# Token order and weight-slot columns in an RWKV-7 / short-convolution layer: every moving slice starts on a multiple of 512 bytes

## The chip, the cores and the metric

The kernel runs on one core of a Trainium2 chip. Five engines work side by side: PE (TensorE, with a second row "PEld" for its weight loads), DVE (VectorE), ACT (ScalarE), POOL (GpSimd) and SP (SyncE, which issues most DMAs). The metric is the device time of one execution in microseconds; the figure of a kernel is the median of its runs.

## The reference, cut to what matters

512 real tokens of width 2048 follow 16 learned meta tokens, so that the layer sees 528. They are normalised and multiplied by one wide matrix `w_in` (2048 x 8320); its columns feed two branches.

```python
h_res = jnp.concatenate([meta, x], axis=1)            # 16 + 512 tokens
hn = _rmsnorm(h_res, norm_in_g[l])
P = hn @ w_in[l]
Pr, Pc = P[..., :RW_COLS], P[..., RW_COLS:]
prev = jnp.pad(Pr[:, :-1], ((0, 0), (1, 0), (0, 0)))
Pr = Pr + (prev - Pr) * mu_shift[l]                   # r, k, v, g, low-rank parts
...
y = _rwkv7_recurrence(rh, decay, kh, vh, kk, kk * ah) # 16 meta frames, then chunks of 64
...
y_b = Bg * _causal_depthwise_conv(Cg * hc, conv_w[l]) * jax.nn.silu(g_c)
mix = jnp.concatenate([y_a, y_b], axis=-1)
h_res = h_res + mix @ w_out[l]
out = _rmsnorm(h_res, norm_f_g)
return out[:, N_META:]
```

Two things of it decide which tokens a column group needs. k, v and the low-rank input ("lora") feed the state from the first meta token on, so they need all 528. r and g need the 512 real tokens and one before them for the shift; C and h need the real tokens and two before them for the convolution of width 3; B and the gate gc need the real tokens alone.

## The kernel before

**The projection.** The 8320 columns of `w_in` are 65 tiles of 128. One tile's product is called a piece: lora, and k, r, v, g, B, C, h, gc with index 0 to 7. `plan` (lines 102 to 107) is their order. The moving operand is the normalised-gain input, split into a high part `xh` and a low part `xl` of 16 rows (one for each 128 input features) of `XROW` = 640 floats, 2560 bytes, of which 528 are tokens. The stationary operand is a 128x128 block of the weights, likewise split into `hi` and `lo`. A block's product is three matmuls, (hi, xh), (hi, xl), (lo, xh), each with a weight load of its own. `steps` (line 320) issues them: for each quarter of a piece (4 of the 16 input rows), for each token range, for each row, the three matmuls.

**Token ranges.** A range is a slice of the moving row and has its own PSUM bank. Tokens lie in time order, meta tokens first. Lines 315 to 318 hold them: `FULL` for k, v and lora, `TAIL` for r and g, `WIDE` for C and h, `REAL` for B and gc. A piece of two ranges has 96 matmuls of 256 to 272 columns, one of `REAL` 48 of 512.

**Weight slots.** Each quarter's weights stand in one of six buffers of `SLOT` = 1152 floats, 4608 bytes (`slot`, line 124): 512 floats of hi and then 512 of lo, shifted inside the slot by `column(j)` floats, which depends on the piece (lines 115 to 119). Rows of 2560 bytes, slots of 4608 and blocks of 512 are all multiples of 512 bytes, so within a piece the distance between where a moving slice begins and where its weights begin is the same modulo 512 bytes for every matmul of a range. In this text **the distance** of a range is (start of the slice - column) x 4 bytes, modulo 512, with the bases of the two pools taken as a multiple of 512 bytes apart.

**Weights on the way.** SP loads half a piece (512 KB) at a time into one of three raw buffers; `split_w` (line 134) casts a quarter to hi on ACT (line 136) and subtracts on DVE or POOL (line 137).

**Out of PSUM.** `scaled` (line 346) multiplies a range by the tokens' norm factors `rs` on DVE, one instruction a range (line 348), and writes a row in time order. `shift_full` and `shift_real` then mix each token with the one before it (ACT and DVE); `use` sends C and h through a product on POOL and the convolution.

**Order.** PE runs in the order in which the program is written; the other engines' order is made by a planner when the kernel is built. The generator `mains` yields one projection matmul at a time, and `fill(ns)` takes projection matmuls until their estimated time (0.43 ns a column) is used up, between the small matmuls of the RWKV branch (lines 563 to 1003). So the projection is what PE does while the branch's chain of DVE, ACT, POOL and DMA steps runs. After the last piece, gc7, a second phase multiplies the mixed branches by `w_out` (line 1234).

**Head.** The first four pieces, lora, k0, r0 and B0, run interleaved while the input arrives. `token_scale_sums` and `token_scale` make `rs`.

Of the kernel before, what the change touches and what calls it, by code (L numbers as in the profile page):

```python
# [13 lines left out]
ALU = mybir.AluOpType  # L14
# [7 lines left out]
SEQ = 512  # L22
META = 16
L = SEQ + META
# [53 lines left out]
def hymba_kernel(ctx: ExitStack, tc: tile.TileContext, xt, xtok, front, w_in, w_out, pv, lup, cst, msk, gf, out):  # L78
    nc = tc.nc
# [35 lines left out]
    def column(j):  # L115
        what, i = plan[j]
        return {
            "k": 8 * i, "v": 8 * i + 56, "r": 8 * i, "g": 8 * i + 56, "C": 8 * i, "h": 8 * i + 56, "B": 8 * i, "gc": 8 * i + 56, "lora": 0,
        }[what]
    stream += [w_out[0, g] for g in range(3)]  # L120
    quarters, chain, low = {}, {}, {}
# [35 lines left out]
    rs = xp.tile([P, L], F32, name="rs")  # L157
# [79 lines left out]
    o = 0  # L237
# [61 lines left out]
    with tc.issue_after(head):  # L299
        nc.vector.tensor_scalar(  # L300
            out=omm, in0=pvt[:, V_MU : V_MU + 33], scalar1=-1.0, scalar2=1.0, op0=ALU.mult, op1=ALU.add
# [10 lines left out]
        )  # L312

    nc.scalar.copy(ones, cs[:, C_BM : C_BM + P + 2])
    FULL = ((0, 256), (256, L))
    TAIL = ((14, 270), (270, L))
    WIDE = ((14, 272), (272, L))
    REAL = ((META, L),)

    def steps(ps, ranges, k4, q, ks=range(4), rs_=range(2)):  # L320
        hi, lo = quarters[q]
# [23 lines left out]

    def scaled(ranges, ps, dst, base):
        for (a, b), p in zip(ranges, ps):
            nc.vector.tensor_tensor(out=dst[:, a - base : b - base], in0=p, in1=rs[:, a:b], op=ALU.mult)

    def shift_full(ps, m, name, dst):  # L350
        pr = cq.tile([P, L + 1], F32, tag="pr", name=f"pr_{name}", bufs=2)
# [42 lines left out]
    def use(what, i, ps):  # L394
        if what == "lora":
            use_lora(ps)
        elif what in ("k", "v"):
            t = cq.tile([P, LP], F32, tag=what, name=f"{what}{i}")
            nc.gpsimd.memset(t[:, META:CH], 0.0)
            shift_full(ps, tile_of[what] + i, f"{what}{i}", padded(t))  # L400
            got[what, i] = t
        elif what in ("r", "g"):
            t = cq.tile([P, SEQ], F32, tag=f"r{i % 2}" if what == "r" else "g", name=f"{what}{i}")
            shift_real(ps, tile_of[what] + i, f"{what}{i}", t)
            if what == "g":
                gate(t, f"r{i}")
                later(14000, lambda: nc.sync.dma_start(gated[i], t))
            got[what, i] = t
        elif what == "C":
            u = tm(f"u{i}")  # L410
            scaled(WIDE, ps, u, 14)
            got[what, i] = u
        elif what == "h":
            u = got["C", i]
            hh = tm(f"hh{i}")
            with behind_of("turned"):
                scaled(WIDE, ps, hh, 14)
            n = SEQ + 2
            nc.gpsimd.tensor_tensor(out=u[:, 0:n], in0=u[:, 0:n], in1=hh[:, 0:n], op=ALU.mult)
            cv = tp.tile([P, SEQ], F32, tag="cw", name=f"cv{i}")  # L420
            nc.scalar.activation(cv, u[:, 0:SEQ], AF.Copy, scale=col(V_CW, i))
            for j in (1, 2):
                nc.vector.scalar_tensor_tensor(
                    out=cv, in0=u[:, j : j + SEQ], scalar=col(V_CW, 8 * j + i), in1=cv, op0=ALU.mult, op1=ALU.add
                )
            got[what, i] = cv
            if i == 0:
                nc.gpsimd.tensor_tensor(out=cv, in0=cv, in1=got["B", 0], op=ALU.mult)
        elif what == "B":
            b = tm(f"b{i}")[:, 0:SEQ] if i else cq.tile([P, SEQ], F32, name="b0")  # L430
            with behind_of("split"):
                scaled(REAL, ps, b, META)
            got[what, i] = b
            if i:
                nc.gpsimd.tensor_tensor(out=got["h", i], in0=got["h", i], in1=b, op=ALU.mult)
        else:
            cv = got["h", i]
            g = tm(f"gc{i}")[:, 0:SEQ]
            scaled(REAL, ps, g, META)
            gate(g, f"c{i}")  # L440
            o = direct.get(8 + i, cv)
            nc.vector.scalar_tensor_tensor(out=o, in0=cv, scalar=0.5, in1=g, op0=ALU.mult, op1=ALU.mult)
            if o is cv:
                later(9000, lambda: nc.sync.dma_start(mixd[8 + i], cv))
        ready.add((what, i))
# [29 lines left out]
    def mains():  # L475
        pa = banks(FULL, "lora", pm, "main")
        pb = banks(FULL, "k0", pz, "tz")
        pc = banks(TAIL, "r0", pm, "main")
        pd = [pi.tile([P, SEQ], F32, tag="ser", name="ps_B0")]
        four = ((pa, FULL), (pb, FULL), (pc, TAIL), (pd, REAL))  # L480
        for k in range(4):
            for n, (ps, rg) in enumerate(four):
                if k == n == 0:
                    hi, lo = quarters[0]
                    for ww, xx, first in ((hi, xh, True), (lo, xh, False), (hi, xl, False)):
                        for p, (a, b) in zip(ps, rg):
                            nc.tensor.matmul(p, ww[:, 0:P], xx[:, 0, a:b], start=first, stop=False)
                            yield (b - a) * 0.43
                    continue
                yield from steps(ps, rg, 0, 2 * n, (k,))  # L490
        for k4 in range(1, 4):
            for n, (ps, rg) in enumerate(four):
                h = 4 * (k4 // 2) + n
                if k4 == 2:
                    prefetch(h + 3)
                if (k4, n) == (3, 2):
                    yb = token_scale_sums()
                if (k4, n) == (3, 3):
                    yield from steps(ps, rg, k4, 2 * h + k4 % 2, range(2))
                    token_scale(yb, 4)  # L500
                    use("lora", 0, pa)
                    use("k", 0, pb)
                    yield from steps(ps, rg, k4, 2 * h + k4 % 2, range(2, 4))
                    continue
                for r in range(2 if n < 3 else 1):
                    if (k4, n, r) == (3, 2, 1):
                        token_scale(yb, 0)
                    yield from steps(ps, rg, k4, 2 * h + k4 % 2, range(4), (r,))
        use("r", 0, pc)
        use("B", 0, pd)  # L510
        for j in range(4, len(plan)):
            what, i = plan[j]
            rg = FULL if what in ("k", "v") else REAL if what in ("B", "gc") else WIDE if what in ("C", "h") else TAIL
            ps = yield from main(j, rg, f"{what}{i}")
            if what == "B" and i < 4:
                state["split"] = low[4 * j + 4]
            use(what, i, ps)
# [794 lines left out]
    for half in range(2):  # L1312
        o = 28 * half
        for g in range(4):
            b = o + 4 + 4 * g
# [134 lines left out]
def _layout(i):  # L1450
    f = np.float32
    x = np.asarray(i["x"])[0]
    hres = np.concatenate([np.asarray(i["meta_tokens"]), x], 0)
    xt = hres.reshape(L, KT, P).transpose(2, 1, 0)
    w = np.asarray(i["w_in"])[0].reshape(KT, P, 65, P).transpose(2, 1, 0, 3).reshape(65, P, DM)

    w, xv, xo = np.array(w), slice(16, 32), slice(0, NPAIR)
    w[xv] = w[xv].reshape(16, P, KT, 2, CH)[:, :, :, ::-1].reshape(16, P, DM)
    wo = np.array(np.asarray(i["w_out"])[0].reshape(KT, 2, CH, 4, 512))
    wo[xo] = wo[xo][:, ::-1]  # L1460
    wo = wo.reshape(8, 2, P, 4, 512).transpose(3, 0, 2, 1, 4).reshape(4, 8, P, 1024)

    def cols(a):
        return np.asarray(a).reshape(-1, P).T

    def swapped(a, first, last):
        a = np.array(cols(a))
        a[:, first:last] = np.roll(a[:, first:last], CH, 0)
        return a

    cw = np.asarray(i["conv_w"])[0]
    pv = np.concatenate(
        [cols(i["norm_in_g"]), swapped(i["mu_shift"], 16, 32)]
        + [cols(i[n]) for n in ("w0", "a0", "k_k", "k_a")]
        + [swapped(i[n], 0, NPAIR) for n in ("lnx_g", "lnx_b")]
        + [cols(i["r_k"])]
        + [cols(cw[j]) for j in range(3)],
        1,
    )
    lup = np.stack([np.asarray(i[n])[0].reshape(64, 8, P) for n in ("w_lora_up", "a_lora_up")], 2)  # L1480
    lup = np.concatenate([lup, lup], 0).transpose(1, 0, 2, 3)

    first = [w[m, :, 0:512].reshape(P, 4, P) for m in (32, 8, 0, 33)]
    front = [pv[:, V_NG : V_NG + KT], first[0][:, 0], xt[:, 0]] + [t[:, 0] for t in first[1:]]
    front += [t[:, 1] for t in first] + [xt[:, 1]] + [t[:, 2:4].reshape(P, 256) for t in first] + [xt[:, 2], xt[:, 3]]
    front = np.concatenate(front, 1)
    cst, msk = _constants()
    return dict(
        xt=xt, xtok=x, front=front, w_in=w, w_out=wo, pv=pv, lup=lup, cst=cst, msk=msk, gf=np.asarray(i["norm_f_g"])
    )  # L1490
# [19 lines left out]
```

## Time and profile before

| | us |
|---|---|
| runs of the kernel | 1026.65, 1027.34, 1027.67 |
| their median | 1027.34 |
| the profiled execution | 1025.72 |
| its span, first to last instruction | 1024.0 |

The mean granted TensorE clock of the profiled execution is 0.998. A row of a group of instructions reads: line, engine, operation, out<-in by the program's names, shapes, count, then busy microseconds and mean nanoseconds of one, then the engine's idle time just before them with what ended it. Matmul durations are modelled and overlap, so a matmul's real price is read from start to start, here called its **pitch**. In the chain of waits a row is start, length and work, and consecutive matmuls of one tile stand as one row with their count; length over count is the pitch. In the timeline a row is start, length, engine, line, operation, tiles, shape and count.

### The profile page before, as it was taken

How to read it: one execution, taken by the hardware profiler on the slowest of the kernel's cores; microseconds unless marked ns; L12 is line 12 of the kernel's file. 1: busy time of each engine (PE TensorE's matmuls, PEld its weight loads, DVE VectorE, ACT ScalarE, POOL GpSimd, SP SyncE). 2: the span in 40 equal slices, each digit the busy share in tenths (PEclk: the TensorE clock that was granted, in tenths of full speed). 3: DMA queues.
4: the chain of work that ended last, by engine and by line, in shares of the span. 5: the costliest groups of instructions: out<-in, count | busy, mean ns of one | idle time of the engine just before them, and what ended most of it. 6: DMA issues, size and time to landing. Idle time of an engine off the chain costs nothing.

```text
span 1024.0 us, 23688 instructions
## 1 busy us (share of the span) xinstructions
PE 1005.1 (98%) x9723; PEld 920.1 (90%) x9723; DVE 685.2 (67%) x1239; ACT 393.4 (38%) x729; POOL 281.2 (27%) x292
## 2 busy tenths in 40 slices
PE   9999999999999999999999999999999999999996
PEld 8899998999988999998999998989889897787875
DVE  7677965587765569555569554244555696998787
ACT  7553423344323434322434322222222335545453
POOL 0122323233232323322423222123332332005001
PEclk9999999999999999999999999999999999999999
DMA  9525576446574363864264855977673697695754
GB/s 324 155 69 145 124 191 173 116 118 150 134 188 130 103 172 88 215 167 117 83 163 100 219 140 166 347 238 232 202 223 95 180 274 180 179 319 139 177 126 165
DMA packets 185036, 174.82 MB, mean 171 GB/s; under 512 B 121568, under 2 KB 142816, under 8 KB 184416
## 3 DMA queue, kind: packets, MB, share of 16 engines
q1 hardware_dynamic: 182336, 164.40, 55.6%
q0 software_dynamic: 2304, 8.39, 4.9%
q8 instruction: 76, 1.25, 0.5%
q10 hardware_dynamic: 288, 0.52, 0.1%
q14 instruction: 32, 0.26, 0.1%
HBM read 136.92 MB, written 36.35 MB: 169 GB/s over the span
## 4 chain that ended last, share of the span: by engine, by line
PE 56%; DVE 8%; DMA 3%; issue 2%; ACT 0%; POOL 0%; DVEq 0%; ACTq 0%; SPq 0%; POOLq 0%
PE ps_gc L329 8%; PE ps_B L329 7%; PE ps_h L329 7%; PE ps_C L329 7%; PE ps_v L329 5%; PE ps_k L329 5%; PE ps_g L329 5%; PE ps_r L329 4%; DVE o L1207 3%; DMA wo<-in_w_out_dram 2%; PE M L1234 2%; PE zs L999 1%; PE zy L1003 1%; PE g L674 1%; DVE xb L1215 1%
## 5 line engine op out<-in xcount | busy, mean ns | idle before, releaser
L137 POOL TENSOR_TENSOR w<-wr,w 128x512 fp32r<-128x512 f32 x119 | 172.2, 1448 | 367.6 <-ACT w L136 307.5
L136 ACT CAST w<-wr 128x512 fp32r<-128x512 f32 x252 | 153.1, 618 | 302.9 <-PE ps_k L329 47.7
L137 DVE TENSOR_TENSOR w<-wr,w 128x512 fp32r<-128x512 f32 x133 | 98.3, 745 | 109.4 <-ACT w L136 98.2
L329 PE MATMUL ps_k<-xh,w 128*128 128x256 f32 (+1 forms) x512 | 96.8, 285 | 1.1 <-DVE w L137 1.1
L329 PE MATMUL ps_v<-xh,w 128*128 128x272 f32 (+1 forms) x512 | 96.5, 285 | 0.0
L329 PE MATMUL ps_r<-xh,w 128*128 128x256 f32 (+1 forms) x512 | 96.4, 283 | 0.0
L329 PE MATMUL ps_h<-xh,w 128*128 128x256 f32 (+1 forms) x512 | 95.2, 284 | 0.0
L329 PE MATMUL ps_C<-xh,w 128*128 128x256 f32 (+1 forms) x512 | 94.1, 282 | 0.0
L329 PE MATMUL ps_g<-xh,w 128*128 128x258 f32 (+1 forms) x512 | 93.4, 282 | 0.0
L329 PE MATMUL ps_B<-xh,w 128*128 128x512 f32 x256 | 84.5, 399 | 0.0
L329 PE MATMUL ps_gc<-xh,w 128*128 128x512 f32 x256 | 82.6, 397 | 0.0
L329 PEld LDWEIGHTS ps_k<-xh,w 128*128 128x128 f32 x512 | 80.4, 188 | 1.8 <-DVE w L137 1.4
L329 PEld LDWEIGHTS ps_r<-xh,w 128*128 128x128 f32 x512 | 80.4, 189 | 0.3
L329 PEld LDWEIGHTS ps_v<-xh,w 128*128 128x128 f32 x512 | 80.4, 188 | 0.3
L329 PEld LDWEIGHTS ps_h<-xh,w 128*128 128x128 f32 x512 | 79.6, 188 | 1.1 <-issue 0.3
L329 PEld LDWEIGHTS ps_C<-xh,w 128*128 128x128 f32 x512 | 79.5, 188 | 0.6
L329 PEld LDWEIGHTS ps_g<-xh,w 128*128 128x128 f32 x512 | 79.4, 189 | 0.3
L329 PE MATMUL ps_v<-xl,w 128*128 128x256 f32 (+1 forms) x256 | 72.8, 284 | 0.0
L329 PE MATMUL ps_k<-xl,w 128*128 128x256 f32 (+1 forms) x256 | 72.8, 284 | 0.0
L329 PE MATMUL ps_g<-xl,w 128*128 128x256 f32 (+1 forms) x256 | 72.6, 284 | 0.0
L329 PE MATMUL ps_r<-xl,w 128*128 128x256 f32 (+1 forms) x256 | 72.4, 283 | 0.0
L329 PE MATMUL ps_h<-xl,w 128*128 128x258 f32 (+1 forms) x256 | 71.9, 281 | 0.2 <-issue 0.2
(321 smaller groups left out, 2272.6 us busy)
## 6 DMA issues: line engine op xcount, KB each, us to landing
wr<-in_w_in_dram SPq DMA_DIRECT2D x126, 512.0 KB
ct<-opd SPq DMA_DIRECT2D x64, 288.0 KB
wo<-in_w_out_dram SPq DMA_DIRECT2D x24, 512.0 KB
x<-in_w_out_dram POOLq DMA_DIRECT2D x16, 512.0 KB, 5.8
opd<-ar SPq DMA_DIRECT2D x8, 576.0 KB
opd<-gt SPq DMA_DIRECT2D x16, 288.0 KB
opd<-bt SPq DMA_DIRECT2D x64, 64.0 KB
x<-in_w_out_dram SPq DMA_DIRECT2D x8, 512.0 KB
```

Source lines behind the costliest of these rows:

```text
L136: nc.scalar.copy(hi, rq)
L137: low[q] = eng.tensor_tensor(out=lo, in0=rq, in1=hi.bitcast(F32), op=ALU.subtract).ins
L329: nc.tensor.matmul(ps[r], ww[:, w], xx[:, kt, a:b], start=(kt == 0 and n == 0), stop=(kt == KT - 1 and n == 2))
L674: nc.tensor.matmul(z[h][:, c - c0], bk[hs, c, h : h + 2, :].rearrange("p a s -> p (a s)"), ar[hs, c].rearrange("p a s -> p (a s)"), start= ...
L999: nc.tensor.matmul(d[hs, j], w, x[hs], start=(a == 0), stop=(a == b - 1))
L1003: nc.tensor.matmul(d[ho, j], t[hs, o : o + CH], x[hs], start=(a == 0), stop=(a == b - 1))
L1207: nc.vector.tensor_tensor(out=lo, in0=rq, in1=hi.bitcast(F32), op=ALU.subtract)
L1215: nc.vector.tensor_tensor(out=h, in0=h, in1=ps, op=op)
L1234: nc.tensor.matmul(bank[s], left(prod, jj, m, s), w, start=(jj == 0 and n == 0), stop=(jj == 7 and n == 2))
```

## The change

The tokens are laid out with the 512 real ones first, then the last two meta tokens, then the first fourteen. Every range now begins at 0 or at 256 floats, a multiple of 512 bytes. The ranges keep 256 + 272 columns for k, v and lora, 256 + 258 for r and g, and 512 for B and gc; C and h, which had 258 + 256, take `TAIL` too and have 256 + 258. `scaled` cuts each range where the token order jumps, so that rows behind it are in time order as before: two ranges of `FULL` take four instructions in place of two, `TAIL` three in place of two, `REAL` one as before. Weight slots are shifted by 16 floats for k, v and lora, by 0 for B and gc, by 8 i for r and C and by 8 i + 64 for g and h.

```diff
@@ column(j)
-            "k": 8 * i, "v": 8 * i + 56, "r": 8 * i, "g": 8 * i + 56, "C": 8 * i, "h": 8 * i + 56, "B": 8 * i, "gc": 8 * i + 56, "lora": 0,
+            "k": 16, "v": 16, "lora": 16, "B": 0, "gc": 0,
+            "r": 8 * i, "g": 8 * i + 64, "C": 8 * i, "h": 8 * i + 64,
@@ ranges
-    FULL = ((0, 256), (256, L))
-    TAIL = ((14, 270), (270, L))
-    WIDE = ((14, 272), (272, L))
-    REAL = ((META, L),)
+    HALF = SEQ // 2
+    FULL = ((0, HALF), (HALF, L))
+    TAIL = ((0, HALF), (HALF, SEQ + 2))
+    REAL = ((0, SEQ),)
+    PLACED = ((0, SEQ, META), (SEQ, SEQ + 2, META - 2), (SEQ + 2, L, 0))
@@ def scaled(ranges, ps, dst, base)
         for (a, b), p in zip(ranges, ps):
-            nc.vector.tensor_tensor(out=dst[:, a - base : b - base], in0=p, in1=rs[:, a:b], op=ALU.mult)
+            for c, d, t in PLACED:
+                c0, d0 = max(a, c), min(b, d)
+                if c0 < d0:
+                    o = t + c0 - c - base
+                    nc.vector.tensor_tensor(
+                        out=dst[:, o : o + d0 - c0], in0=p[:, c0 - a : d0 - a], in1=rs[:, c0:d0], op=ALU.mult
+                    )
@@ use, mains: C and h
-            scaled(WIDE, ps, u, 14)
+            scaled(TAIL, ps, u, 14)
...
-            rg = FULL if what in ("k", "v") else REAL if what in ("B", "gc") else WIDE if what in ("C", "h") else TAIL
+            rg = FULL if what in ("k", "v") else REAL if what in ("B", "gc") else TAIL
@@ def _layout(i)
-    hres = np.concatenate([np.asarray(i["meta_tokens"]), x], 0)
+    meta = np.asarray(i["meta_tokens"])
+    hres = np.concatenate([x, meta[META - 2 :], meta[: META - 2]], 0)
```

The distances that follow, in bytes, by the definition above (i is the piece's index):

| pieces | before, the two ranges | after, both ranges |
|---|---|---|
| lora, k | 512 - 32 i | 448 |
| v | 288 - 32 i | 448 |
| r | 56 - 32 i | 512 - 32 i |
| g | 344 - 32 i | 256 - 32 i |
| C | 56 - 32 i, 64 - 32 i | 512 - 32 i |
| h | 344 - 32 i, 352 - 32 i | 256 - 32 i |
| B | 64 - 32 i | 0 |
| gc | 352 - 32 i | 0 |

(each modulo 512). The moving slices of r, g and the first of C and h began at 56 or 1080 bytes, those of B and gc at 64.

More of the change, by code (lines that the diff above doesn't have):

```diff
@@ L416, in use @@
             with behind_of("turned"):
-                scaled(WIDE, ps, hh, 14)
+                scaled(TAIL, ps, hh, 14)
             n = SEQ + 2
```

## The prediction

> **What bounds the kernel now.** I read the page, then the busy time by stage, then PE's waits.
>
> ```profile
> span 1024.0 us, 23688 instructions
> ...
> PE 1005.1 (98%) x9723; PEld 920.1 (90%) x9723; DVE 685.2 (67%) x1239; ACT 393.4 (38%) x729; POOL 281.2 (27%) x292
> ```
> ```profile
> 56.00:170.00 114.00, 113.50 (x919) 109.37 (x917) 80.61 (x166) 42.60 (x80) 33.19 (x39) 1.00 0.56 140
> 170.00:330.00 160.00, 157.31 (x1682) 149.40 (x1683) 110.70 (x216) 58.38 (x109) 51.55 (x55) 1.00 0.54 144
> 330.00:630.00 300.00, 300.00 (x2804) 286.68 (x2804) 188.82 (x382) 105.74 (x193) 91.52 (x92) 1.00 0.54 141
> 630.00:811.00 181.00, 180.76 (x2988) 160.22 (x2986) 83.61 (x139) 49.76 (x94) 54.50 (x46) 1.00 0.71 221
> 811.00:857.00 46.00, 46.00 (x292) 41.52 (x291) 39.68 (x55) 16.23 (x31) 16.76 (x10) 1.00 0.86 232
> ```
> ```profile
> PE t L846 <- DVE xn L837: 2.0, 1, 2.0
> ...
> PE ps_k L329 <- DVE w L137: 1.1, 1, 1.1
> ```
>
> The columns of the second view are stretch, length, PE, PEld, DVE, ACT and POOL busy (with counts), granted clock, DMA share, GB/s. From 56 to 857 us PE is busy in 797.6 of 801 us at a granted clock of 1.00, and its two longest waits are 2.0 and 1.1 us. No other engine comes near. The matmuls' pitch sets this stretch, so a nanosecond on a projection matmul goes to the end. What follows hangs on the last piece:
>
> ```profile
> 844.90 11.17 PE ps_gc L329 x48
> ...
> 856.09 0.69 DVE gc L348
> ...
> 859.04 5.49 DMA x<-in_w_out_dram
> ```
>
> In the chain of waits gc7 frees DVE at 856.09, and after the gate a DMA is issued at 859.04 for which the second phase waits. An earlier gc7 moves all of this earlier.
>
> **The pitch, and what the distance does to it.** These are rows of the chain; length over count is the pitch.
>
> ```profile
> 328.31 11.79 PE ps_k L329 x96
> ...
> 341.67 2.40 PE ps_r L329 x20
> ...
> 352.61 8.70 PE ps_v L329 x72
> ...
> 392.16 11.78 PE ps_v L329 x96
> ...
> 458.24 8.16 PE ps_B L329 x35
> ...
> 471.25 8.83 PE ps_gc L329 x37
> 480.08 11.73 PE ps_k L329 x96
> ...
> 543.83 11.73 PE ps_v L329 x96
> ...
> 609.87 8.36 PE ps_B L329 x35
> ...
> 622.98 8.62 PE ps_gc L329 x37
> 631.60 11.41 PE ps_C L329 x96
> ...
> 799.56 11.24 PE ps_gc L329 x48
> 810.80 11.44 PE ps_C L329 x96
> 822.25 11.44 PE ps_h L329 x96
> 833.69 11.21 PE ps_B L329 x48
> ```
>
> B2 (458.24) and B3 (609.87) are cut at the same points by the same small matmuls; only the distance differs, 0 against 480 bytes. The pitch is 233.1 against 238.9 ns. gc3 (622.98, distance 256) against gc2 (471.25, 288) gives 233.0 against 238.6. So the pitch does depend on the distance, by 5.7 ns in 235. The Trainium skill, "SBUF — State Buffer", section "Who interferes with whom", gives PE two independent read ports, one for the moving operand and one for weight loads, and says that PE never waits on anyone; by it the distance would do nothing. The two pairs disagree, and the measurement decides.
>
> With 256 columns the pitch has several stable values:
>
> ```profile
> 145.22 0.28 PE L329 MATMUL ps_C<-xl,w 128*128 128x256 f32 x1
> ...
> 146.24 0.28 PE L329 MATMUL ps_C<-xl,w 128*128 128x256 f32 x1
> ```
> ```profile
> 172.05 0.29 PE L329 MATMUL ps_k<-xl,w 128*128 128x272 f32 x1
> ...
> 173.17 0.29 PE L329 MATMUL ps_k<-xl,w 128*128 128x272 f32 x1
> ...
> 173.88 0.28 PE L329 MATMUL ps_k<-xl,w 128*128 128x256 f32 x1
> ...
> 174.59 0.28 PE L329 MATMUL ps_k<-xl,w 128*128 128x256 f32 x1
> ...
> 178.05 0.28 PE L329 MATMUL ps_k<-xl,w 128*128 128x256 f32 x1
> ...
> 178.73 0.28 PE L329 MATMUL ps_k<-xl,w 128*128 128x256 f32 x1
> ```
>
> Every third matmul reads xl, so between two such rows lie 9, 9, 6 and 6 matmuls. C0 (distance 64) runs at 1.02/9 = 113 ns. k2 already stands where the change puts all of k and v, at 448 bytes with column 16 and ranges from 0 and 256: its 272 columns take 1.12/9 = 124 ns, its 256 columns 0.71/6 = 118 ns in one group and 0.68/6 = 113 ns in another, the latter just after small matmuls had broken in. One distance thus holds two rhythms, and which one holds depends on what ran before.
>
> **The sum, part by part.**
>
> B and gc go to distance 0. B2 and gc3 have that pitch already; 13 pieces gain 5.7 ns x 48 = 0.27 us each: **3.5 us**. The least I take is 2.5 (some of the 13 are near it already), the most 4.0.
>
> k and v: k4, k6, v5 and v7 take 11.79, 11.73, 11.78 and 11.73, mean 11.76 us. At k2's values a piece is 48 x (118 + 124) = 11.62 us in the slower rhythm and 48 x (113 + 124) = 11.38 in the faster; halfway, 11.50, gains 0.26. v4 (352.61) has 120.8 ns, 11.60 a piece, and is no worse than the middle; with k2, k3 and v3, which stand at or within one step of 448 or of v4's 160, I count it as nothing. 11 pieces x 0.26 = **2.8 us**; ends 1.5 and 4.2.
>
> r and g begin at 56 bytes now and have 120 ns whatever the width (341.67: 2.40/20). C and h have one such range and one of 256 columns on a multiple of 64 bytes, and 11.41 and 11.44 us a piece, a pair of 238.3 ns, so the aligned range has about 118.3. After the change r and g are built like that. 15 pieces (r0 is in the head) x 48 x 1.7 ns = **1.2 us**. For 258 columns from 256 no row exists; the nearest are k's 272 columns (124 ns, which at equal excess is 118) and the unaligned 120. I take 120, since their mean over distances is nearer it. Ends: 31 pieces x 48 x 2 ns, 3.0 us either way. C0 loses its 113: 48 x 5 ns = **-0.25 us**.
>
> The head: lora, k0 and B0 are of the same kind, 2 x 0.26 + 0.27 = 0.8 us, of which I count half, **0.4**, as the wait for `rs` stands behind them.
>
> DVE gets 2 more instructions for each of 17 pieces and 1 more for each of 32: 66. The nearest row is a copy of 16 columns out of PSUM:
>
> ```profile
> L473 DVE COPY rs<-prs 128x16 f32<-128x16 f32 x1 | 0.2, 174 | 0.2 <-PE prs L472 0.2
> ```
>
> At 0.174 us that is 11.5 us of DVE time at most, against 1024.0 - 685.2 = 338.8 idle. It lies beside PE's next piece (11 us); a PSUM bank is written again two pieces later. If that cover were gone, all 11.5 us would show. No DMA and no wait of SP's or POOL's queue is moved.
>
> Not all of PE's gain survives, since other engines' steps do not shrink:
>
> ```profile
> 61.54 0.70 DVE L387 TENSOR_TENSOR la<-lora_th,la 64x528 fp32r<-64x528 f32 x1
> ```
> ```profile
> 62.30 0.39 PE L564 MATMUL tz<-la,luh 128*128 128x272 f32 x1
> ```
>
> DVE ends `la` at 62.24 and PE takes it at 62.30: v0's share before it, 52 matmuls x 2.6 ns, becomes a wait of 0.15 us, and lora's and k0's four small pieces may add 0.4. Before the 2.0 us wait for xn nothing on PE since the last gram matmuls (37 us before) helps: 0.9% of 37, 0.3 us. Together **-0.8 us**, ends 0 and 3.
>
> Sum: 3.5 + 2.8 + 1.2 - 0.25 + 0.4 - 0.8 = 6.85 us, 0.7%. The profiled span goes from 1024.0 to 1017.2; its execution has 1.7 us around it, 1018.9; the median of the runs lies 1.6 above that execution: **1020.5 us**.
>
> **The rivals.**
>
> *The distance is worth less than the pairs say.* The pairs were measured with slices that began at 64 bytes and columns that were not 0; if only B and gc answer, and k and v stay in the slower rhythm, 3.5 us remain less 0.5 of waits: **1024.3**. For it: k2's first groups at 118 ns. Against it: v4's 120.8.
>
> *The distance does nothing for the end.* PE saves, and waits for DVE steps that have not moved: **1027.3**. For it: the matmul at 62.30 comes at once behind `la`. Against it: the 300 us from 330 to 630 without any idle time. The port rule quoted above would end here too; the pairs speak against it.
>
> *Every rhythm is the fast one.* With 256 columns at 113 ns throughout (C0, k2), k and v gain 4.2, and r, g, C and h 46 x 48 x 5 = 11 us: with half of the latter, 3.5 + 4.2 + 5.5 - 1, **1015**. The Trainium skill, "TensorE: Matmul & The Clock Gate", section "Back-to-back issue gap", has N/2.4 + 2.5 ns, 109 ns for 256 columns; no row here gets below 113.
>
> *Slower: weights come late.* The planner puts the added DVE pieces ahead of weight splits on DVE; PE then starves as k2 did at 1.1 us (line 137, in the waits above). Each such stall costs 1.1 us, so from seven on the gain is gone; at ten the time is 1020.5 + 11, **1031.5**. Against it: PE leaves a quarter every 2.9 us (11.7/4) and six buffers stand between, so a split of 0.7 us must be some 10 us late.
>
> **How the numbers follow.** The forecast (gain 4 to 10 us) has 0.60, the weak gain 0.14, nothing 0.09, every rhythm fast 0.08, slower 0.09. What a measurement of this kernel can tell from no change is about 0.2%, 2 us. Faster is 0.60 + 0.14 + 0.08 = 0.82, same 0.09, slower 0.09. The parts' ends, 2.5 + 1.5 - 1.8 and 4.0 + 4.2 + 4.2 before waits, and the neighbours put the range at **1015.5 to 1026**; beyond it lie the slower case and parts of two others.
>
> **What would show it.** B's and gc's pitch in stretches without breaks is near 233 or less in every piece; whole k and v pieces take 11.4 to 11.6 us; r and g come to 11.4; PE still shows no wait over 2 us before 857. It is wrong if B's pitch stays at 234 or more, if 258 columns exceed 121 ns, or if PE waits for line 137 or 348 appear by the dozen.

## The result, and the profile after

| | median, us | runs | ratio to before, with its 95% interval |
|---|---|---|---|
| before | 1027.51 | 1026.65 to 1028.28 (4) | |
| after | 1022.37 | 1021.18 to 1022.86 (4) | 0.9948 [0.9931, 0.9966] |

The change saves 5.1 us, half a per cent. The profiled execution of after took 1022.35 us; against the profiled execution of before, 1025.72, that is only 3.4 us. The two differ in the granted clock as well, 0.995 against 0.998, and this will matter below.

First the head of the page of after and its busy time by stage (stretch, length, then busy PE, PEld, DVE, ACT and POOL, granted clock, DMA share, GB/s).

```profile
span 1020.6 us, 23761 instructions
...
PE 1001.5 (98%) x9723; PEld 919.9 (90%) x9723; DVE 688.1 (67%) x1305; ACT 393.9 (39%) x729; POOL 274.8 (27%) x292
```
```profile
170.00:330.00 160.00, 157.56 (x1678) 149.63 (x1679) 110.83 (x228) 57.70 (x109) 46.28 (x55) 0.99 0.54 144
330.00:630.00 300.00, 300.00 (x2822) 286.93 (x2821) 191.43 (x411) 107.00 (x196) 91.20 (x92) 1.00 0.54 143
```

PE still sets the time. It has as many matmuls as before, is still busy in all 300 us from 330 to 630, and does 2822 of its records there in place of 2804: the same work at a shorter pitch. DVE has the 66 added instructions and only 2.9 us more busy time than before. In the stage before, the clock is 0.99 and no longer 1.00.

Then the rows of the chain of waits (start, length, work) that answer to those of before.

```profile
328.76 11.58 PE ps_k L331 x96
...
341.92 2.39 PE ps_r L331 x20
...
352.87 8.65 PE ps_v L331 x72
...
392.06 11.54 PE ps_v L331 x96
...
457.53 8.16 PE ps_B L331 x35
...
470.48 8.62 PE ps_gc L331 x37
479.10 11.59 PE ps_k L331 x96
...
542.04 11.53 PE ps_v L331 x96
...
607.68 8.16 PE ps_B L331 x35
...
620.61 8.62 PE ps_gc L331 x37
629.23 11.55 PE ps_C L331 x96
...
797.47 10.89 PE ps_gc L331 x48
808.35 11.36 PE ps_C L331 x96
819.72 11.36 PE ps_h L331 x96
831.08 10.90 PE ps_B L331 x48
841.98 10.89 PE ps_gc L331 x48
```

B2 and B3 both take 8.16 us now, gc2 and gc3 both 8.62; before, one of each pair was slower. Whole B and gc pieces take 10.89 or 10.90 where they took 11.17 to 11.24: 226.9 ns a matmul against 233 to 234. k and v come from 11.73 to 11.79 down to 11.53 to 11.59. C and h are no better as a group: C4 (629.23) went up from 11.41 to 11.55, C7 and h7 down from 11.44 to 11.36. gc7 ends at 852.87, 3.2 us earlier than the 856.07 of before.

PE's waits (engine, what waits, for whom; us in all, times, longest):

```profile
PE t L854 <- DVE xn L845: 2.2, 1, 2.2
...
PE ps_k L331 <- DVE w L138: 1.1, 1, 1.1
PE ps_h L331 <- issue: 0.8, 1, 0.8
...
PE ps_gc L331 <- DVE w L138: 0.2, 1, 0.2
```

No wait for weights by the dozen has appeared. The wait for `xn` went from 2.0 to 2.2 us; h6's 0.8 and gc's 0.2 are small. What the waits do not show stands behind the first of them, in PE's timeline (start, length, work; in brackets the wait):

```profile
306.81 1.12 PE L854 MATMUL t<-xn,gt 64*64 64x64 f32 x32 [2.17 <-DVE xn L845]
...
307.86 0.79 PE L331 MATMUL ps_B<-xh,w 128*128 128x512 f32 x1
...
308.45 0.63 PE L331 MATMUL ps_B<-xl,w 128*128 128x512 f32 x1
308.88 1.05 PE L331 MATMUL ps_B<-xh,w 128*128 128x512 f32 x2
309.73 0.63 PE L331 MATMUL ps_B<-xl,w 128*128 128x512 f32 x1
```

From 308.45 to 309.73 lie three matmuls: 427 ns each instead of 228. The granted clock is halved for 3.4 us from 306.9, and once more for 3.4 us from 863.3, behind a wait of 1.7 us for ACT, which had itself waited for a DMA. The profile of before has neither, although its wait for `xn` was nearly as long (2.01 us).

### The profile page after: what moved, and what is told of

It is laid out like the page before. It is cut to its first block, busy times and chain, and to the rows that moved or that the text cites. A ratio compares the mean times of both kernels' runs of the same rounds, so it can differ in the third digit from the quotient of the medians.

```text
span 1020.6 us, 23761 instructions
## 1 busy us (share of the span) xinstructions
PE 1001.5 (98%) x9723; PEld 919.9 (90%) x9723; DVE 688.1 (67%) x1305; ACT 393.9 (39%) x729; POOL 274.8 (27%) x292
## 4 chain that ended last, share of the span: by engine, by line
PE 56%; DVE 8%; DMA 3%; issue 3%; ACT 1%; POOL 0%; DVEq 0%; ACTq 0%; SPq 0%; POOLq 0%
PE ps_gc L331 8%; PE ps_B L331 7%; PE ps_h L331 7%; PE ps_C L331 7%; PE ps_v L331 5%; PE ps_g L331 5%; PE ps_k L331 5%; PE ps_r L331 4%; DVE o L1215 3%; DMA wo<-in_w_out_dram 2%; PE M L1242 2%; PE zs L1007 1%; PE zy L1011 1%; PE rz L955 1%; PE g L682 1%
## 5 line engine op out<-in xcount | busy, mean ns | idle before, releaser
L138 POOL TENSOR_TENSOR w<-wr,w 128x512 fp32r<-128x512 f32 x119 | 165.4, 1390 | 368.7 <-ACT w L137 317.1
L331 PE MATMUL ps_h<-xh,w 128*128 128x258 f32 (+1 forms) x512 | 95.3, 284 | 0.0
L331 PE MATMUL ps_C<-xh,w 128*128 128x258 f32 (+1 forms) x512 | 94.4, 283 | 0.0
L331 PE MATMUL ps_h<-xl,w 128*128 128x256 f32 (+1 forms) x256 | 72.2, 282 | 0.8 <-issue 0.8
```

What stands on the lines that cost most here:

```text
L138: low[q] = eng.tensor_tensor(out=lo, in0=rq, in1=hi.bitcast(F32), op=ALU.subtract).ins
L331: nc.tensor.matmul(ps[r], ww[:, w], xx[:, kt, a:b], start=(kt == 0 and n == 0), stop=(kt == KT - 1 and n == 2))
```

## The experiments

"Steady pitch" is my own evaluation of the traces: the mean of start to start of consecutive projection matmuls in stretches without breaks, by piece and width. The "excess" of a kernel is the sum over all these pairs of (pitch - columns/2.4), in us; it is what the pitch costs beyond streaming. Before has 64.86 us of it, after 58.97.

**Before once more, unchanged.** How much of a profile's difference is chance?

> The kernel before, unchanged, for a second profile. If its first profiled execution (1025.72 us, clock 1.00 throughout) was a lucky one, this one is near 1027.5 us and shows one or two stretches of some 3.4 us at half clock behind PE's waits near 305 and 865 us, some 1.3 us each, as the changed kernel's profile does. If the clock is not what separates them, it shows no such stretch and the same projection pitches, and the 1.8 us lie elsewhere.

One run: 1025.16 us, span 1023.4, clock 0.997. The excess is 64.85 us against 64.86 in the first profile of before, and there is no stretch at half clock. Before's summed pitch thus repeats to 0.01 us, and that of after, which was profiled twice as well (58.97 and 59.22), to 0.25. The time of a run does not repeat as well: 15 runs of before taken beside this one go from 1026.12 to 1028.30. A second measure that repeats is the time from v0's first matmul to gc7's last, here called the **main stretch**: 799.62 and 799.63 us in the two profiles of before. v0's first matmul itself starts at 56.04 and 55.73, so the head moves by 0.3 us by chance.

**The distance alone, without the new order.** The tokens stay in time order, ranges begin where they did, `scaled` is the old one; only the columns change, so that k, v and lora stand at 448 bytes, B and gc at 0, r and g at 448, C and h at 440 (258 columns) and 448 (256).

```diff
@@ against before
-            "k": 8 * i, "v": 8 * i + 56, "r": 8 * i, "g": 8 * i + 56, "C": 8 * i, "h": 8 * i + 56, "B": 8 * i, "gc": 8 * i + 56, "lora": 0,
+            "k": 16, "v": 16, "lora": 16, "B": 16, "gc": 16,
+            "r": 30, "g": 30, "C": 32, "h": 32,
```

> The old token order and ranges, only the columns changed: k, v, lora, B and gc to 16, so that k and v keep distance 448 and B and gc distance 0 with slices that begin at 64 bytes; r and g to 30 (distance 448 from starts at 56 bytes), C and h to 32 (440 and 448). Distance theory: B and gc at 227 to 229 ns, k and v at 113 to 118 and 123.5 ns, the gain of the change is here too, about 5.5 us, 1022 us; C's and h's aligned range gains 1 to 3 ns more (up to 2 us); r and g stay at 120 ns or fall to 116 if an even start does not matter. Rival, that slices must begin on multiples of 512 bytes: B and gc stay near 233 ns and the time near 1027.

1021.14 us (1019.78 to 1022.94, 5 runs), 0.9937 [0.9924, 0.9951]. The excess is 58.97, the same as after's. The main stretch takes 796.07 us, in the profile of after above 796.56. This profile too has the two stretches at half clock, from 306.6 and 863.0, so the new order is not needed for them. From its chain of waits:

```profile
328.34 11.58 PE ps_k L330 x96
...
391.60 11.53 PE ps_v L330 x96
...
796.36 10.88 PE ps_gc L330 x48
807.24 11.40 PE ps_C L330 x96
...
830.05 10.91 PE ps_B L330 x48
840.95 10.90 PE ps_gc L330 x48
```

k, v, B and gc are as fast as in after, with B's slices at 64 bytes and k's row order untouched. So the columns give as much as the whole change, without the new token order and the 66 DVE instructions. One thing the distance does not do here: r and g, whose slices begin at 56 and 1080 bytes, stay at 120 ns at distance 448, where C's and h's 256 columns, which begin at 1088 bytes, have 116.5 and 116.7.

**The order alone.** After, with the columns of before.

```diff
@@ against after
-            "k": 16, "v": 16, "lora": 16, "B": 0, "gc": 0,
-            "r": 8 * i, "g": 8 * i + 64, "C": 8 * i, "h": 8 * i + 64,
+            "k": 8 * i, "v": 8 * i + 56, "r": 8 * i, "g": 8 * i + 56, "C": 8 * i, "h": 8 * i + 56, "B": 8 * i, "gc": 8 * i + 56, "lora": 0,
```

> The new token order and ranges with the old columns. Distance theory: B and gc keep a mean of 232 ns, k and v of 118 and 125.4; r and g fall from 120 to 118 ns in their 256 columns (-1 us) and the 258 columns rise by 1 ns (+1.3 us): no change, 1027 to 1028 us. Rival, that starts on 512 bytes bring the gain: 1022.4 us.

1026.19 us (1024.46 to 1028.63, 11 runs), 0.9993 [0.9984, 1.0002]: no difference that can be told. The excess is 64.02, 0.8 below before; the main stretch takes 799.30 us, 0.3 below before. Its chain:

```profile
327.77 11.80 PE ps_k L330 x96
...
391.67 11.78 PE ps_v L330 x96
...
799.02 11.19 PE ps_gc L330 x48
...
833.14 11.19 PE ps_B L330 x48
```

The k, v, B and gc pieces have the lengths of before. The order does bring r's and g's 256 columns from 120.1 to 117.9 and 117.5 ns, but their 258 columns, now from float 256, go from 119.5 to 120.1. It also carries the 66 added DVE instructions of after, and shows that they cost nothing that can be told.

**All of r, g, C and h at 448.** After, with one column for them.

```diff
@@ against after
-            "r": 8 * i, "g": 8 * i + 64, "C": 8 * i, "h": 8 * i + 64,
+            "r": 16, "g": 16, "C": 16, "h": 16,
```

> The changed kernel with r, g, C and h at column 16 too, distance 448 in all pieces of two ranges. Distance theory: their 256 columns fall from a mean of 118 ns to the 114 to 116 that C2, h2 and r2 show at 448 and 192, 31 pieces x 48 x 3 ns = 4 us, so 1018 us. Rival, that C2 and r2 are good by what runs before them and not by distance: 1022.4 us.

1018.22 us (1017.24 to 1018.89, 4 runs), 0.9913 [0.9899, 0.9926]; excess 54.56. That is 4.4 us of pitch below after. C's, g's and h's 256 columns run at 114.5 to 114.9 ns, r's at 116.1; the 258 columns stay at 120.3. Over the sixteen distances of the change the mean is 117.7 to 118.3, so they cost against one good one. Beside the columns-only kernel it shows what moving the starts off 56 and 1080 bytes does at the same distance of 448: r's and g's 256 columns go from 120.2 and 120.1 ns to 116.1 and 114.9.

**A sweep of distances.** Each piece a column of its own; B and gc cover 15 distances of 512 columns, r, g, C and h others of 256.

```diff
@@ against after
-            "k": 16, "v": 16, "lora": 16, "B": 0, "gc": 0,
-            "r": 8 * i, "g": 8 * i + 64, "C": 8 * i, "h": 8 * i + 64,
+            "k": 16, "v": 16, "lora": 16,
+            "B": (0, 1, 2, 4, 8, 16, 32, 64)[i], "gc": (12, 24, 48, 96, 80, 112, 127, 124)[i],
+            "r": (16, 12, 13, 14, 15, 17, 18, 20)[i], "g": (22, 24, 11, 10, 9, 19, 21, 23)[i],
+            "C": (14, 15, 17, 18, 12, 20, 13, 19)[i], "h": (4, 28, 36, 44, 52, 60, 6, 80)[i],
```

> Columns differ from piece to piece in steps down to 4 bytes: B1 to B7 at 1, 2, 4, 8, 16, 32, 64 floats, gc0 to gc7 at 12, 24, 48, 96, 80, 112, 127, 124, r, g, C and h mostly at 9 to 24. If only the exact distance counts, B1 (508 bytes) already has 233 ns and the 256 columns beside column 16 lose the 114 to 116 at once; if the pattern is smooth and repeats after 256 bytes, B1, gc6 (4 bytes) and B7 (256) keep 227 to 229 ns and columns 14 to 18 stay under 117. Time 1019 to 1024.

One run, 1022.78 us. The steady pitch by distance, worked out from its trace (0 from after, 448 of 256 columns from the kernel above):

| distance in bytes | 512 columns, ns | | distance in bytes | 256 columns, ns |
|---|---|---|---|---|
| 0 | 228.0 | | 436 | 113.7, 114.6 |
| 4 | 233.2 | | 448 | 114.8 |
| 16 | 226.7 | | 192 | 114.4 |
| 256 | 227.2 | | 460 | 115.4 |
| 496 | 228.5 | | 456, 440, 444 | 118.0, 118.4, 118.6 |
| 320, 64 | 228.9, 229.9 | | 452, 432 | 119.7, 119 |
| 504, 508 | 230.5, 232.4 | | 272, 400 | 119.0, 120.1 |
| 128, 384, 448, 464, 480, 192, 416 | 232.2 to 234.0 | | 488 | 121.1 |
| | | | 304, 336, 368, 416, 420, 424, 428, 464, 468, 472, 476, 496 | 116.5 to 119.9 |

Four rows of the chain of this kernel carry the ends: gc6 at 4 bytes, C7 at 436, B7 at 256 and gc7 at 16.

```profile
797.67 11.20 PE ps_gc L333 x48
808.87 11.24 PE ps_C L333 x96
...
831.38 10.91 PE ps_B L333 x48
842.28 10.89 PE ps_gc L333 x48
```

Neither picture holds: it isn't one exact distance that is good, and pitch isn't smooth in the distance. For 512 columns 0, 16, 256 and 496 are all near 227 to 228.5, and a single float off zero costs 3.4 ns in B1 (508 bytes) and 6.5 ns in gc6 (4 bytes), each against the same piece at 0 in after. For 256 columns the good places are few (436, 448, 192, 460), with poor ones 4 to 12 bytes beside them. A good place for one width isn't one for another: 448 bytes is poor for 512 columns.

Two things limit the table. Each of its rows is one piece or two, and pieces at one distance differ: at 0 bytes in after from 226.7 ns (gc6, gc7) to 229.1 (B4), at 448 bytes in the kernel above from 114.8 for C to 117.3 for k. Rows closer than that are not ranked by it. And it varies the weights' address alone; that the distance counts, and not where the weights begin, is seen beside the columns-only kernel: B5 has column 16 in both, and takes 233.3 ns here with slices from 0 (distance 448), 228.5 there with slices from 64 bytes (distance 0).

**The wait for xn filled.** Does the half clock come from the wait? In after, more projection matmuls are put ahead of those that wait for the third `xn`.

```diff
@@ against after
-        fill(FW["tr"])
+        fill(FW["tr"] + (2600 if first == 2 else 0))
```

> The changed kernel with 2600 ns more projection matmuls put ahead of the second pair's matmuls that wait for xn (PE's 2.2 us wait near 304). Theory that this wait costs itself and, by a half-clock stretch of 3.4 us behind it, some 1.3 us more: the wait goes to under 0.5 us, no stretch at half clock stands near 306, and the time falls from 1022.4 by 2 to 3.5 us, to 1019 to 1020.5. Rival, that the chain behind it (pair 2's inverse, then pair 3) is late next and takes the time back: 1022.

1018.19 us (1016.93 to 1019.31, 5 runs), 0.9912 [0.9897, 0.9927]. Against after's 1022.37 that is 4.2 us less, more than the wait itself. Windows of the first profile of after and of this kernel around the place:

```profile
304.00:312.00 8.00, 5.83 (x78) 4.80 (x78) 3.45 (x4) 2.11 (x4) 3.12 (x3) 0.79 0.48 151
861.00:868.00 7.00, 5.10 (x15) 3.85 (x15) 5.32 (x8) 5.90 (x10) 0.89 (x1) 0.76 0.59 161
```
```profile
300.00:312.00 12.00, 11.95 (x169) 9.29 (x169) 8.42 (x9) 5.44 (x11) 5.96 (x5) 1.00 0.55 157
```

Without the wait PE is busy in 11.95 of 12 us there and the clock is 1.00; all five runs have a mean clock of 0.998. The second stretch at half clock, from 863, is gone as well in this profile, though nothing was done there. The second profile of after (the last experiment) has neither stretch although the wait is in place, so one profile doesn't show what starts them. Against that profile, with the full clock in both, the fill brings 2.1 us at the wait. The span is 3.2 us shorter, but 1.05 us of it lies in the head, 300 us before the place of the edit; why is not known.

**The same fill with all of r, g, C and h at 448.**

```diff
@@ against after
-            "r": 8 * i, "g": 8 * i + 64, "C": 8 * i, "h": 8 * i + 64,
+            "r": 16, "g": 16, "C": 16, "h": 16,
...
-        fill(FW["tr"])
+        fill(FW["tr"] + (2600 if first == 2 else 0))
```

> The same added projection matmuls in the kernel with all two-range pieces at distance 448. By the same theory 1018.2 falls to 1015 to 1016.5 us; by the rival it stays at 1018.

1015.03 us (1013.85 to 1015.54, 4 runs), 0.9883 [0.9865, 0.9900]. The two steps, 4.1 us for the column and 4.2 for the fill, would add up to 8.3; together they bring 7.3. The profile of the kernel without the fill has one stretch at half clock, from 306.1, and this one none: here the fill brings 3.7 us at the place, 1.6 more than the 2.1 without such a stretch. Yet the mean clock of these four runs is 0.997 three times and 0.996 once, against 0.996 three times and 0.998 once without the fill: that the fill raises the mean clock is plain in the kernel before this one, hardly here.

**The best distance of the sweep.** The kernel before this one, with r, g, C and h at column 19, 436 bytes.

```diff
@@ against the kernel before this one
-            "r": 16, "g": 16, "C": 16, "h": 16,
+            "r": 19, "g": 19, "C": 19, "h": 19,
```

> The kernel with 2600 ns more ahead of xn, and r, g, C and h at column 19 (distance 436) in place of 16. If the 113.7 and 114.6 ns that g5 and C7 showed there hold for all, the 31 pieces' pairs go from 235.1 to 233.2 to 234.1 ns, 1.5 to 3 us less than 1015.0: 1012 to 1013.5. If those two were lucky in what ran before them, 1015 to 1018.

1012.34 us (1011.75 to 1013.36, 4 runs), 0.9852 [0.9833, 0.9870]; excess 52.70. The 256 columns run at 113.9 to 114.5 ns, the 258 at 119.5 to 119.6.

**And k, v and lora too.**

```diff
@@ against the kernel before this one
-            "k": 16, "v": 16, "lora": 16, "B": 0, "gc": 0,
+            "k": 19, "v": 19, "lora": 19, "B": 0, "gc": 0,
```

> The same with k, v and lora at column 19 too. Their 256 columns stand at 117.3 and 116.1 ns and the 272 at 123.5 with column 16. If 436 bytes suit the 256 columns whatever stands beside them, they go to 114 and 1 to 2 us more are gained (1011 to 1012.5); if the 272 columns have a worse rhythm there (125 to 127 ns), as most distances have, the time is 1 to 2 us above the other kernel's.

1009.67 us (1008.84 to 1010.19, 4 runs), 0.9824 [0.9806, 0.9842]; excess 50.38. It is the fastest of the kernels here, 17.4 us below before (1027.09, measured beside it). Its chain:

```profile
383.40 11.37 PE ps_v L331 x96
420.89 11.20 PE ps_C L331 x96
...
469.55 11.37 PE ps_k L331 x96
...
806.63 11.20 PE ps_h L331 x96
```

k and v take 11.37 us with 113.9 ns for 256 columns and 123.2 to 123.4 for 272; at 448 bytes they took 11.53 to 11.59.

**After once more, unchanged.**

> The changed kernel once more, on the same chip as these. 1021.2 to 1022.9 us; runs whose mean granted clock is 0.998 would be near 1020, those at 0.995 near 1022.5.

1022.32 us (1020.08 to 1023.56, 6 runs), 0.9948 [0.9930, 0.9966], as the first time. The one run at a mean clock of 0.998 took 1020.25, the two at 0.995 took 1022.49 and 1023.4, as expected; those at 0.996 took 1022.14 and 1023.56. The profiled execution took 1020.08, with a span of 1018.3. Its windows:

```profile
304.00:312.00 8.00, 5.83 (x143) 4.70 (x143) 4.12 (x5) 2.73 (x5) 3.10 (x3) 1.00 0.50 164
861.00:868.00 7.00, 7.00 (x32) 5.76 (x32) 7.00 (x9) 6.41 (x10) 0.89 (x1) 1.00 0.58 135
```

The same program, with PE waiting as long (5.83 of 8 us busy in both), has a clock of 1.00 here: 143 matmuls, many of them small, lie in the 8 us instead of 78. Up to 300 us the main stretch runs alike in both profiles of after, to 0.1 us; behind 312 us the first is 1.5 us late, which is what the stretch at half clock cost it. The last projection matmul group, gc7, starts its last matmul at 850.49, against 852.47 in the first profile of after and 855.66 in before. The main stretch takes 794.66 us, and the excess is 59.22.

## Why the prediction was right, and where it was off

The forecast was 1020.5 us; the kernel takes 1022.4, inside the range and faster, as forecast, by 5.1 us in place of 6.85. The second profile of after, without a stretch at half clock, is the one to lay beside the sum: its last projection matmul starts 5.2 us earlier than in before. 5.0 us of that is the main stretch: 5.6 us less pitch, and 0.7 more in waits and breaks. The other 0.2 is the head, no more than the 0.3 by which the two profiles of before differ there. That the median lies 1.6 us above a profiled execution was taken from one profile; for after's two it is 0.0 and 2.2, so how near the forecast came to the median is in part luck.

| term | forecast, us | measured, us (steady pitch, after against before) |
|---|---|---|
| B and gc at 0 | 3.5 | 3.1: 232.4 and 232.0 ns to 228.0 and 227.7 |
| k and v at 448 | 2.8 | 2.4: 272 columns 125.4 to 123.5, 256 columns 117.8 to 117.2 (k) and 118.3 to 116.2 (v) |
| r and g | 1.2 | 1.0: 256 columns +1.5, 258 columns -0.5 |
| C and h | -0.25 | -0.45: 256 columns +0.25, 258 columns -0.7 |
| head | 0.4 | none that can be told: v0 starts at 55.91 and 55.84, before at 56.04 and 55.73 |
| waits that do not shrink | -0.8 | -0.7 in the second profile of after |

The four pitch terms add up to 6.05 us because they count all 48 matmuls of a range; the 5.6 us count only those in stretches without breaks.

*What bounds it* was right: 5.0 of the 5.6 us of pitch reached gc7, and from gc7's last matmul on the kernel takes as long as it did (168.3 and 168.0 us before, 168.1 and 167.8 after). *The pairs of the chain* (B2 against B3, gc3 against gc2) gave the distance's worth nearly: the two are equal now, and the other 13 pieces gained 5.1 ns on average in place of 5.7. gc1 gained only 1.2, since it stood near the good pitch already, the others 4.2 to 7.5. (The means in the table are over 15 pieces, B2 and gc3 among them.) *k2 as the pattern for k and v* was right for the 272 columns, 124 ns; the 256 columns stayed nearer the slower of its two rhythms, so the middle, 11.50 us, was missed by 0.06 a piece. *DVE's 66 instructions at nothing* was right. The two new forms at the edges of a range, in the groups by line:

```profile
L354 DVE TENSOR_TENSOR pr_k<-ps_k,rs 128x14 f32<-128x14 f32 x8 | 1.3, 160 | 0.0
...
L354 DVE TENSOR_TENSOR pr_r<-ps_r,rs 128x2 f32<-128x2 f32 x8 | 1.2, 147 | 0.0
```

At 147 to 160 ns, 66 of them are some 10 us of DVE time, and the kernel with the order alone carries them without a loss.

*The term that was mis-sized* is the 258 columns from 256, taken at nothing: they went from 119.5 to 120.0 in r and to 120.4 to 120.6 in g, C and h, 1.2 us over 31 pieces, still under the 121 named as the bound. The kernel with the order alone shows the same 120.1 to 120.6 with other columns, but the order is not all of it: in the old order the new columns bring C's and h's 258 columns to 120.2, and in the new order column 19 brings all of them back to 119.5. The distance has a part in it, and the two were not taken apart.

*The waits* were sized well. Of the signs named, one failed by a little: PE was to show no wait over 2 us, and the wait for xn went from 2.0 to 2.2, as the term of 0.3 us for it had it. One thing behind the wait wasn't seen: a stretch at half clock follows it in some executions. It cost the first profile of after 1.5 us against the second; six matmuls at 427 ns in place of 228 are 1.2 of them, the small matmuls on xn the rest. The second stretch, from 863, adds only 0.3 us to the span. In runs of equal mean clock the gain seems larger: at 0.998 before takes 1026.1 us (mean of 12 runs) and the one such run of after 1020.25, so 5.9. By this single run the clock takes back almost 1 us at the medians; that is not shown. The runs with the wait filled fit it: 4.2 us for a wait worth 2.1 and up to two such stretches.

*The rivals.* That the distance does nothing for the end fell with the columns-only kernel. The weak gain, 1024.3, is as far from the measured time as the forecast, but its condition doesn't hold: k and v answered, and r and g too. "Weights come late" did not occur: line 138 holds PE up once for 1.1 us, as before, and once for 0.2. "Every rhythm is the fast one" is not what this change reaches, but the place exists: at 436 bytes all 256-column ranges run at 114 ns.

What the title says of the change isn't what pays. Slices on a multiple of 512 bytes gave nothing that can be told by themselves; the columns alone gave as much as the change. What the starts do bring is r's and g's ranges off 56 and 1080 bytes: 1.5 us in the change, and 3.4 at 448 bytes (7 x 48 x 4.1 + 8 x 48 x 5.2 ns). A multiple of 512 isn't needed for most of that: C's and h's ranges from 1088 bytes have 116.5 and 116.7 at 448. In r and g the weights' start goes with the slices' there (from 120 to 64 bytes into the slot); which of the two counts was not taken apart.

The Trainium skill, "SBUF — State Buffer", section "Who interferes with whom", gives PE two independent read ports and says that it never waits on anyone, by which the distance would do nothing; two kernels with the same instructions and other columns differ by 6 us, and the measurement decides. Open is the mechanism: no run here tells why the pitch depends on single floats of distance, why the good places differ with the width, or how two rhythms can hold at one distance. Whether the clock halves behind a wait was not controlled either, only taken away with the wait.

## What to carry to other kernels

Where PE streams without a break, lay the address of the stationary operand against that of the moving one and measure the pitch by piece: a shift of a few floats in a slot cost nothing and was worth 3% of a 512-column matmul (234 to 227 ns) and 6% of a 256-column one (121 to 114), and it must be measured for each width, in one sweep with a different shift in each piece, the best of which is then tried in all pieces. Try the shift alone before rearranging data for it. Take a wait of 2 us on PE as up to 3.7 us, since the clock halved behind it in some profiles here, and compare profiles at equal clock before believing a difference of half a per cent.

## What the runs showed of the hardware that was not expected

**The pitch by single floats.** One float off distance zero brings gc6's 512 columns from 226.7 to 233.2 ns; 16 bytes off is as good as zero (226.7 in gc7 at both). C3's 256 columns take 118.4 ns at 440 bytes and 113.8 at 436, in the kernel with column 19. Nothing in these pieces' instructions differs but the weights' address.

**The half clock comes in some executions and not in others.** One program, after, with the same wait of 2.2 us, had the clock halved for 3.4 us in one profile and not in the other; neither profile of before has it behind a wait of 2.0, and that of the columns-only kernel has it behind 2.1. Over 35 runs of before the time follows the mean granted clock: 1026.1 us at 0.998 (12 runs), 1027.2 at 0.997 (8), 1028.1 at 0.996 (13), 1029.9 at 0.995 (2). The mean clock accounts for four fifths of the variance between these runs. That stretches at half clock made the slower ones slow is not shown, since both profiles of before are of quick executions (1025.72 and 1025.16 us) without one. And the mean clock is not all: the five runs with the wait filled, all at 0.998, go from 1016.93 to 1019.31.
